# A transformer stack in split fp32: one weight tile of each stage multiplies old residual and new part apart, while the norm is made

## The chip, the cores and the metric

One core of a Trainium2 chip runs the whole network in one launch. TensorE (PE in the rows) multiplies, VectorE (DVE) and ScalarE (ACT) do the elementwise work, GpSimd (POOL) a few small steps, SyncE (SP) issues the loads of weights. The metric is the device time of one launch in microseconds, the median of several runs.

## What is computed

A batch of one, 256 tokens and 16 meta tokens (272 columns), a model width of 1024, depth 2. Layer 0: half-step SwiGLU, neighbourhood attention, half-step SwiGLU. Layer 1: the same with differential attention. Then a hybrid mixer (attention and an mLSTM side by side) and a squared-ReLU mlp. Every sublayer has a norm ahead and a norm behind:

```
def rmsnorm(x, g):
    xf = x.astype(jnp.float32)
    y = xf * lax.rsqrt(jnp.mean(xf * xf, axis=-1, keepdims=True) + RMS_EPS)
    return (y * g.astype(jnp.float32)).astype(x.dtype)

def swiglu(x, w_gate, w_up, w_down):
    return (jax.nn.silu(x @ w_gate) * (x @ w_up)) @ w_down

...
        f1 = swiglu(rmsnorm(h, g[0]), ffn_w_gate[i, 0], ffn_w_up[i, 0], ffn_w_down[i, 0])
        h = h + FFN_RES * rmsnorm(f1, g[1])
        j = i // N_MIXERS
        hn = rmsnorm(h, g[2])
```

The last lines tell the pattern: the residual h gets the sublayer's output, normed by its own mean square, and the next sublayer takes h, normed again.

## The kernel before, in words

The residual lies transposed, as `h[128, 8, 272]`: eight blocks of 128 features on the partitions, tokens on the columns (272 in the first four stages told of below, `ALL`; 256 behind them, `GRID`, where the meta tokens are no longer needed). Weights come as tiles of 128x1024 (one output block, eight input blocks) into `wr`. ACT rounds a tile to a high part `wh` (L156), DVE makes the remainder `wl` (L168). Inputs are split in the same way into `xh` and `xl`. A full product of an input block with a weight tile is three matmuls: wh·xh, wh·xl, wl·xh (L393 to L395); 24 for a tile. `W` is the ring of weight tiles: `W.next` takes one, `W.done` frees it, `W.pump`, `W.high` and `W.low_if` issue the loads and splits of coming ones at places in the program that are written by hand. The order on every engine is the order in which the code records the operations.

The norm ahead of a sublayer is not applied to its input. `xh` and `xl` hold g·h, the product is made with that, and the scale 1/rms, `rb`, is multiplied in when the product is taken out of PSUM. `rb` is needed only there, so its row sums (`Norm.head`) and transposes (`Norm.tail`) are put inside the next two gemms, behind a block that `first` and `second` name. The norm behind a sublayer is `Post`: `evac(ps, j)` takes the output of block j into `f` (times its gain) and adds its squares to a sum; `finish` makes the scale `bc` from it, by a ones-matmul over the partitions (L344), a mean (L356), a power on POOL (L349) and a transpose back (L368 to L373); then h += f·bc for each block (`addend` L617, `block` L623).

Between the last matmul of a sublayer and the first of the next stands this chain. `start_phase` is the piece of code for it, and it is called seven times: at about 214 us (neighbourhood mixer), 358 (ffn), 563 (ffn), 769 (differential mixer), 907 (ffn), 1099 (hybrid mixer) and 1236 us (mlp). While the chain runs, PE does idle matmuls on weights (`turn_over`, L476), nine between the row sums and the transposes, nine behind these. Then DVE forms block after block of h, ACT rounds it to `xh` (L436), DVE the low parts `xl` (L453), and PE multiplies four weight tiles block by block: for each block the high products of four tiles (L502, L503), at the end all low ones (L506): 4 x 24 = 96 matmuls. Behind them stand the sums of squares for `rb`.

The stages at 214, 563, 769 and 1099 follow `down`, the last gemms of an ffn: eight output blocks in pairs, each of three weight tiles. Those at 358, 907 and 1236 follow `proj_out`, which has one tile for each block, four blocks begun together as the attention's heads come out, and then the other four one by one. Attention's last steps stand in the code behind the start of `proj_out`, as it waits for its heads one by one.

Of the kernel before, what the change touches and what calls it, by code (L numbers as in the profile page):

```python
# [10 lines left out]
F32 = mybir.dt.float32  # L11
FR = mybir.dt.float32r
I32 = mybir.dt.int32
AF = mybir.ActivationFunctionType
# [7 lines left out]
T = S + NM  # L22
# [11 lines left out]
NK = NM + 4 * KC  # L34
HK = NK // 2
R_BUFS = 3


def constants():
# [170 lines left out]
def block_kernel(ctx: ExitStack, tc: tile.TileContext, a, out):  # L210
# [13 lines left out]
    def nm(s):  # L224
        uid[0] += 1
        return f"{s}_{uid[0]}"
# [149 lines left out]
    def square_into(acc, src, j, cols, bias=0.0, engine=dve):  # L376

        if j == 0:
            act.activation(acc[:, cols], src, AF.Square, bias=bias)
            return None  # L380
        q = tmp("sq")
        if j == NB - 1:
            x = cols.start
            for a, b in ((x, x + 128), (x + 128, T)):
                act.activation(q[:, a:b], src[:, a - x:b - x], AF.Square, bias=bias)
            return q
        act.activation(q[:, cols], src, AF.Square, bias=bias)  # L387
        engine.tensor_tensor(acc[:, cols], acc[:, cols], q[:, cols], op=OP.add)  # L388
# [34 lines left out]
    class Norm:  # L423


        def __init__(self, g, cols):
            self.g, self.cols = g, cols
            self.xh = bp.tile([128, 8, T], FR, name=nm("xh"), tag="xh", bufs=1)
            self.xl = bp.tile([128, 8, T], FR, name=nm("xl"), tag="xl", bufs=1)
            self.x = (self.xh, self.xl)  # L430
            self.acc = tp.tile([128, T], F32, name=nm("accp"), tag="acc", bufs=1)
# [6 lines left out]
        def square(self, j):  # L438
            c = self.cols
            q = square_into(self.acc, h[:, j, c], j, c, engine=pool)  # L440
            if q is not None:
                pool.tensor_tensor(self.acc[:, c], self.acc[:, c], q[:, c], op=OP.add)

        def sum(self, sq):

            c = self.cols
            dve.tensor_tensor(sq[:, 0:4, c], sq[:, 0:4, c], sq[:, 4:8, c], op=OP.add)
            dve.tensor_tensor(sq[:, 0:2, c], sq[:, 0:2, c], sq[:, 2:4, c], op=OP.add)
            dve.tensor_tensor(self.acc[:, c], sq[:, 0, c], sq[:, 1, c], op=OP.add)

        def low(self, j):
            c = self.cols
# [9 lines left out]
            act.activation(self.rb[:, self.cols], p[:, self.cols], AF.Copy)  # L462
            return self.rb

    def start_phase(norm, post, n=4):

        c = norm.cols
        w = [W.next() for _ in range(n)]  # L470
        ps = [ps_mm() for _ in range(n)]

        def turn_over(m):
            x = w[0][0].rearrange("p a b -> p (a b)")[:, 0:256]
            for _ in range(m):
# [3 lines left out]
        for k in range(2):  # L479
            act.activation(old[k][:, c], h[:, k, c], AF.Copy, scale=norm.g[:, k:k + 1])  # L480
        post.finish(turn_over)
        turn_over(9)
        t = []
        for k in range(2):
            t.append(post.addend(k))
            dve.scalar_tensor_tensor(norm.xh[:, k, c], t[k][:, c], norm.g[:, k:k + 1], old[k][:, c],
                                     op0=OP.mult, op1=OP.add)
        for k in range(2, 8):
            post.block(k)
            norm.block(k)  # L490
        for k in range(2):
            dve.tensor_tensor(h[:, k, c], h[:, k, c], t[k][:, c], op=OP.add)
        squares = post.f
        for x, y in ((2, 6), (6, 8), (0, 2)):
            act.activation(squares[:, x:y, c], h[:, x:y, c], AF.Square)
            if x:
                W.high()
        for k in range(8):
            norm.low(k)
        for k in range(8):  # L500
            for q in range(n):
                pe.matmul(ps[q][:, c], w[q][0][:, k, :], norm.xh[:, k, c], start=k == 0, stop=False)  # L502
                pe.matmul(ps[q][:, c], w[q][1][:, k, :], norm.xh[:, k, c], start=False, stop=False)  # L503
        for k in range(8):
            for q in range(n):
                pe.matmul(ps[q][:, c], w[q][0][:, k, :], norm.xl[:, k, c], start=False, stop=k == 7)  # L506
        W.low_if()
        norm.sum(squares)
        W.done(n)
        return ps  # L510

# [77 lines left out]
    class Post:  # L589


        def __init__(self, g, cols, bias=None, gbias=None):
            self.g, self.cols, self.bias, self.gbias = g, cols, bias, gbias
# [15 lines left out]
        def finish(self, between=lambda n: None):  # L609
            r = rstd_head(self.m, self.cols, self.sq)  # L610
            between(9)
            self.bc = rstd_tail(r, self.cols)

        def addend(self, j):
# [10 lines left out]
    def down(post, x_of, kbs):  # L625
        c = post.cols
        W.flush()
        for m2 in range(4):
            ps = [ps_mm(), ps_mm()]
            for n, kb in enumerate(kbs):  # L630
                last = n == len(kbs) - 1
                for q in range(2):
                    gemm(ps[q], x_of(n), c, kb, n == 0, last)
                    if last:
                        post.evac(ps[q], 2 * m2 + q)
                    if not (last and m2 == 3):
                        W.pump()
# [50 lines left out]
    def proj_out(post, x, order=range(8)):  # L688

        c = post.cols  # L690
        w = [W.next() for _ in range(4)]
        ps = [ps_mm() for _ in range(4)]
        for n, k in enumerate(order):
            while k not in ready:
                assert bg_list
                bg()
            W.flush()
            for q in range(4):
                mm3(ps[q][:, c], w[q], k, x, k, c, n == 0, n == 7)
# [189 lines left out]
        mask_bias(1)  # L889
        yield  # L890

    post = Post(half_gains(0, 1), ALL)
    bg_list.append(prepare())
    ffn(n0, post, (meta0, turn0, high0, keep0, gains_in, post.f), first_phase)

# [36 lines left out]
    QT = [slice(NM, NM + 128), slice(NM + 128, T)]  # L932


    norm = Norm(gains(0, 2), ALL)
    kq = slot(5, F32, "kq")
    Oh, Ol = slot(0, FR, "Oh"), slot(1, FR, "Ol")
    e_slot = slot(4, F32, "keep").rearrange("p a b -> p (a b)")
# [212 lines left out]
            mask_bias(2 + n // 8)  # L1151

    mixer(norm, post, na_evac, na_attention, ALL, na_before)
    post = Post(gains(0, 3), ALL, vgain("b_o"), gbo)
    proj_out(post, (Oh, Ol))


    norm = Norm(gains(0, 4), ALL)
    post2 = Post(half_gains(0, 5), ALL)
    t5b = []  # L1160

    def load_t5():
# [8 lines left out]

    bg_list.append(load_t5())
    ffn(norm, post2, post)
    norm = Norm(gains(1, 0), ALL)
    post = Post(half_gains(1, 1), ALL)
    ffn(norm, post, post2)


    norm = Norm(gains(1, 2), ALL)
    kq = slot(5, F32, "kq")  # L1180
    Oh, Ol = slot(0, FR, "Oh"), slot(1, FR, "Ol")
    keep_in(slot(3, F32, "keep"), slot(4, F32, "keep"))
# [109 lines left out]
                yield  # L1292

    mixer(norm, post, da_evac, da_attention, GRID, lambda n: None)
    post = Post(gains(1, 3), GRID)
    proj_out(post, (Oh, Ol))

    norm = Norm(gains(1, 4), GRID)
    post2 = Post(half_gains(1, 5), GRID)
    ffn(norm, post2, post)  # L1300


    norm = Norm(vgain("mix_pre"), GRID)
    Oh, Ol = slot(0, FR, "Oh"), slot(1, FR, "Ol")
    qk = slot(2, F32, "qk")
    vt = slot(3, F32, "vt")
# [11 lines left out]
    c = GRID  # L1318

    act.preload_act_table_set("natural_log_exp_and_others")  # L1320
    pg, *ps4 = start_phase(norm, post2)
# [244 lines left out]
    for n, (kind, i) in enumerate(plan):  # L1566
# [27 lines left out]
            bg_list.append(mlstm())  # L1594
            bg_list.append(causal_attention())
        bg()
    post = Post(vgain("mix_post"), GRID)
    proj_out(post, (Oh, Ol), [4, 5, 6, 7, 0, 1, 2, 3])


    norm = Norm(vgain("mlp_pre"), GRID)
    before = post
    uh = [slot(i, FR, "uh") for i in range(4)]
    ul = [slot(4 + i, FR, "ul") for i in range(4)]
# [117 lines left out]
```

## Time and profile before

| | |
|---|---|
| median of three runs | 1431.84 us (1429.91 to 1431.91) |
| the profiled run | 1431.22 us |
| its span, first to last instruction | 1429.4 us |
| PE busy | 1408.2 us, 99% |
| DVE busy | 893.7 us, 63% |
| ACT busy | 750.2 us, 52% |
| POOL busy | 168.1 us, 12% |
| mean granted TensorE clock | 0.998 |

Busy shares are means over the span. At the places that matter here PE's row of 99% holds the idle matmuls of the seven stages too, which are busy and do nothing. A time of one instruction is read with care where a row has several: they overlap, and the busy time over the count is the step from one to the next.

### The profile page before, as it was taken

How to read it: one execution, taken by the hardware profiler on the slowest of the kernel's cores; microseconds unless marked ns; L12 is line 12 of the kernel's file. 1: busy time of each engine (PE TensorE's matmuls, PEld its weight loads, DVE VectorE, ACT ScalarE, POOL GpSimd, SP SyncE). 2: the span in 40 equal slices, each digit the busy share in tenths (PEclk: the TensorE clock that was granted, in tenths of full speed). 3: DMA queues.
4: the chain of work that ended last, by engine and by line, in shares of the span. 5: the costliest groups of instructions: out<-in, count | busy, mean ns of one | idle time of the engine just before them, and what ended most of it. 6: DMA issues, size and time to landing. Idle time of an engine off the chain costs nothing.

```text
span 1429.4 us, 26895 instructions
## 1 busy us (share of the span) xinstructions
PE 1408.2 (99%) x11068; PEld 1357.6 (95%) x11068; DVE 893.7 (63%) x1668; ACT 750.2 (52%) x1333; POOL 168.1 (12%) x185
## 2 busy tenths in 40 slices
PE   9999999999999999999999999999999999999997
PEld 9999999899999999999999888999999888899886
DVE  6776447664865544955546785776555877686542
ACT  5554346666554444644445564664444565676441
POOL 1325001010221200212100001031100000000000
PEclk9999999999999999999999999999999999999999
DMA  7875552352575554555553352375554543275650
GB/s 250 271 251 172 179 185 66 124 167 90 167 229 172 168 180 148 175 180 177 163 182 99 119 177 89 112 244 184 188 178 131 177 129 108 89 234 179 221 177 30
DMA packets 219528, 234.41 MB, mean 164 GB/s; under 512 B 5313, under 2 KB 209894, under 8 KB 219214
## 3 DMA queue, kind: packets, MB, share of 16 engines
q1 hardware_dynamic: 218206, 227.38, 49.2%
q0 software_dynamic: 656, 4.94, 1.1%
q8 instruction: 87, 1.43, 0.4%
q10 hardware_dynamic: 544, 0.38, 0.1%
q14 instruction: 35, 0.29, 0.1%
HBM read 231.62 MB, written 5.13 MB: 166 GB/s over the span
## 4 chain that ended last, share of the span: by engine, by line
PE 91%; DVE 6%; ACT 2%; DMA 1%; issue 1%; POOL 0%; DVEq 0%; POOLq 0%; ACTq 0%; SPq 0%
PE pm L393 24%; PE pm L395 24%; PE pm L394 23%; PE ps L1645 2%; PE ps L1644 2%; PE ps L1646 2%; PE pm L506 2%; DVE wl L168 2%; PE pm L502 2%; PE pm L503 1%; DMA wr<-in_da_w_qkv_dram 1%; PE pt L344 1%; PE pt L1013 1%; PE pm L540 1%; PE ps L1022 1%
## 5 line engine op out<-in xcount | busy, mean ns | idle before, releaser
L168 DVE TENSOR_TENSOR wl<-wr,wh 128x1024 fp32r<-128x1024 f32 (+1 forms) x430 | 514.3, 1204 | 122.9 <-ACT wh L156 122.2
L393 PE MATMUL pm<-xh,wh 128*128 128x272 f32 (+1 forms) x1992 | 581.4, 292 | 2.2 <-DVE Ol L421 2.2
L395 PE MATMUL pm<-xh,wl 128*128 128x272 f32 (+1 forms) x1992 | 570.4, 286 | 0.0
L394 PE MATMUL pm<-xl,wh 128*128 128x272 f32 (+1 forms) x1992 | 568.5, 285 | 0.0
L156 ACT ACTIVATE wh<-wr 128x1024 fp32r<-128x1024 f32 (+1 forms) x430 | 440.7, 1033 | 194.0 <-PE pm L394 112.9
L393 PEld LDWEIGHTS pm<-xh,wh 128*128 128x128 f32 x1992 | 376.0, 189 | 11.2 <-issue 9.4
L395 PEld LDWEIGHTS pm<-xh,wl 128*128 128x128 f32 x1992 | 375.9, 189 | 0.1
L394 PEld LDWEIGHTS pm<-xl,wh 128*128 128x128 f32 x1992 | 375.6, 189 | 0.1
L395 PE MATMUL pm<-mh,wl 128*128 128x272 f32 (+1 forms) x704 | 202.2, 287 | 0.0
L393 PE MATMUL pm<-mh,wh 128*128 128x272 f32 (+1 forms) x704 | 202.1, 287 | 0.0
L394 PE MATMUL pm<-ml,wh 128*128 128x272 f32 (+1 forms) x704 | 201.5, 286 | 0.0
L650 POOL TENSOR_TENSOR sr<-sl,rb 128x272 f32<-128x272 f32 (+1 forms) x88 | 104.5, 1192 | 320.1 <-ACT sl L648 320.1
L395 PEld LDWEIGHTS pm<-mh,wl 128*128 128x128 f32 x704 | 132.7, 188 | 0.0
L394 PEld LDWEIGHTS pm<-ml,wh 128*128 128x128 f32 x704 | 132.6, 188 | 0.0
L393 PEld LDWEIGHTS pm<-mh,wh 128*128 128x128 f32 x704 | 132.6, 188 | 0.0
L420 ACT ACTIVATE mh<-m 128x272 fp32r<-128x272 f32 (+1 forms) x88 | 37.7, 428 | 117.8 <-DVE m L655 117.6
L655 DVE TENSOR_TENSOR m<-pm,sr 128x272 f32<-128x272 f32 (+1 forms) x88 | 38.3, 435 | 80.5 <-PE pm L395 74.8
L648 ACT ACTIVATE sl<-gq 128x272 f32<-128x272 f32 (+1 forms) x88 | 36.9, 427 | 95.8 <-DVE gq L646 95.6
L349 POOL TENSOR_TENSOR s<-s,mhalf 128x3 f32<-128x3 f32 (+1 forms) x15 | 19.1, 1274 | 558.4 <-DVE s L362 336.1
L646 DVE TENSOR_TENSOR gq<-pm,rb 128x272 f32<-128x272 f32 (+1 forms) x88 | 37.6, 435 | 71.6 <-PE pm L395 69.0
L388 DVE TENSOR_TENSOR accf<-accf,sq 128x272 f32<-128x272 f32 (+1 forms) x42 | 18.3, 436 | 81.9 <-ACT sq L387 81.8
L502 PE MATMUL pm<-xh,wh 128*128 128x272 f32 (+1 forms) x224 | 56.7, 291 | 0.6
(337 smaller groups left out, 1728.6 us busy)
## 6 DMA issues: line engine op xcount, KB each, us to landing
wr<-in_ffn_w_gate_dram SPq DMA_DIRECT2D x43, 1024.0 KB
wr<-in_ffn_w_up_dram SPq DMA_DIRECT2D x43, 1024.0 KB
wr<-in_ffn_w_down_dram SPq DMA_DIRECT2D x32, 1024.0 KB
wr<-in_w_up_dram SPq DMA_DIRECT2D x16, 1024.0 KB
wr<-in_w_down_dram SPq DMA_DIRECT2D x16, 1024.0 KB
wr<-in_ffn_w_down_dram SPq DMA_DIRECT2D x16, 768.0 KB
wr<-in_na_w_qkv_dram SPq DMA_DIRECT2D x12, 1024.0 KB
wr<-in_da_w_qkv_dram SPq DMA_DIRECT2D x12, 1024.0 KB
```

The costliest lines, as they stand in the source:

```text
L156: self.nc.scalar.activation(hi, w, AF.Copy)
L168: engine.tensor_tensor(lo, w, hi.bitcast(F32), op=OP.subtract)
L393: pe.matmul(ps, wh[:, k, :], xh[:, j, cols], start=start, stop=False)
L394: pe.matmul(ps, wh[:, k, :], xl[:, j, cols], start=False, stop=False)
L395: pe.matmul(ps, wl[:, k, :], xh[:, j, cols], start=False, stop=stop)
L420: act.activation(hi, src, AF.Copy)
L502: pe.matmul(ps[q][:, c], w[q][0][:, k, :], norm.xh[:, k, c], start=k == 0, stop=False)
L506: pe.matmul(ps[q][:, c], w[q][0][:, k, :], norm.xl[:, k, c], start=False, stop=k == 7)
L646: dve.tensor_tensor(t[:, c], ps[:, c], norm.rb[:, c], op=OP.mult)
L648: act.activation(s[:, c], t[:, c], AF.Silu)
L650: pool.tensor_tensor(s2[:, c], s[:, c], norm.rb[:, c], op=OP.mult)
L655: dve.tensor_tensor(t[:, c], ps[:, c], gated.pop(f)[:, c], op=OP.mult)
```

## The change

One of the four tiles of a stage, the `early` one (the first; in the hybrid mixer the second), takes its input blocks 0 to 3 in two terms. g·h_new is g·h_old + bc·(g·f), so W·(g·h_new) is W·(g·h_old) + bc·W·(g·f). Both products can be made before `bc` is known. `Norm.ahead` rounds and splits g·h_old of blocks 0 to 3 and g·f of blocks 0 to 3 into the columns of `xh` and `xl` that the stage fills later (blocks 0 to 3 and 4 to 7). PE makes 12 matmuls of the new part into a bank `term` and 12 of the old into the tile's own bank, in place of the 18 idle ones: 11 (256 columns: 10) between the row sums and the transposes, 10 behind these, the rest behind the first block. `term` is copied out by ACT, multiplied by `bc` and added at the end of the stage on DVE (`scaled`, `fb`). The early tile then needs only its blocks 4 to 7. So that these come first, the order of the blocks is 4, 5, 6, 7, 0, 1, 2, 3.

The copies and subtractions of h are recorded by `Post.next_norm`: in `down` at its second pair of blocks, in `proj_out` at its start. Those of f are recorded in `evac` behind blocks 4 and 5, two blocks each. A weight split (`W.low_if`) is recorded behind block 6. `head` moves from behind block 3 to behind block 6 of the first gemm after the stage, `tail` from block 1 to block 5 of the second. The new norm's sums of squares stand ahead of the stage's last weight split.

```
+ORDER = (4, 5, 6, 7, 0, 1, 2, 3)
+LOWS = (6, 7, 4, 5, 0, 1, 2, 3)
...
-            self.first, self.second = {3: self.head}, {1: self.tail}
+            self.first, self.second = {6: self.head}, {5: self.tail}
...
+        def ahead(self, j, src, x):
+            c = self.cols
+            act.activation(self.xh[:, x + j, c], src[:, j, c], AF.Copy, scale=self.g[:, j:j + 1])
+            dve.scalar_tensor_tensor(self.xl[:, x + j, c], src[:, j, c], self.g[:, j:j + 1],
+                                     self.xh[:, x + j, c].bitcast(F32), op0=OP.mult, op1=OP.subtract)
...
-    def start_phase(norm, post, n=4):
+    def start_phase(norm, post, n=4, early=0):
...
-        def turn_over(m):
-            x = w[0][0].rearrange("p a b -> p (a b)")[:, 0:256]
+        term = ps_mm()
+        def products():
+            for x, into in ((4, term), (0, ps[early])):
+                for k in range(4):
+                    for i, (part, v) in enumerate(((0, norm.xh), (1, norm.xh), (0, norm.xl))):
+                        pe.matmul(into[:, c], w[early][part][:, k, :], v[:, x + k, c],
+                                  start=k == 0 and i == 0, stop=x == 4 and k == 3 and i == 2)
+                        yield
...
-                pe.matmul(ps[0][:, 0:256], x[:, 0:128], x, start=True, stop=True)
...
-        post.finish(turn_over)
-        turn_over(9)
+        post.finish(lambda: some(11 if c is ALL else 10))
+        some(10)
+        scaled = tp.tile([128, T], F32, name=nm("fs"), tag="fs", bufs=1)
+        act.activation(scaled[:, c], term[:, c], AF.Copy)
...
+        def tiles(k):
+            return [q for q in range(n) if k > 3 or q != early]
...
+        high(ORDER[0])
+        some(24)
+        for k in ORDER[2:]:
             post.block(k)
             norm.block(k)
...
+        dve.tensor_tensor(scaled[:, c], scaled[:, c], post.bc[:, c], op=OP.mult)
...
+        for k in ORDER[1:]:
+            high(k)
...
+        norm.sum(squares)
         W.low_if()
-        norm.sum(squares)
+        x = tmp("fb")
+        dve.tensor_tensor(x[:, c], scaled[:, c], ps[early][:, c], op=OP.add)
+        ps[early] = x
...
+            if j in (4, 5):
+                for k in range(2):
+                    self.norm.ahead(2 * (j - 4) + k, self.f, 4)
+            if j == 6:
+                W.low_if()
+        def next_norm(self):
+            self.norm = Norm(self.gain, self.cols)
+            for j in range(4):
+                self.norm.ahead(j, h, 0)
...
+            if m2 == 1:
+                post.next_norm()
...
         ps = [ps_mm() for _ in range(4)]
+        post.next_norm()
```

On DVE, at the end of neighbourhood attention (330 us), the order before was this; `lg` and `s` are the masked logits and their maxima, `ps` the bank that PE filled, `Ol` the low part of a finished head.

```order
L421 TENSOR_TENSOR Ol_2578<-ps_4024,Oh_2577 128x256
L923 ISA lg_4141,s_4142<-ps_4134,bt_2770 128x176
L923 ISA s_4142 128x1
L923 ISA lg_4145,s_4146<-ps_4135,bt_2770 128x176
L923 ISA s_4146 128x1
```

and is now, the lines moved by the added code:

```order
L423 TENSOR_TENSOR Ol_2594<-ps_4040,Oh_2593 128x256
L451 SCALAR_TENSOR_TENSOR xl_4145<-h,G,xh_4144 128x272 x4
L968 ISA lg_4167,s_4168<-ps_4160,bt_2789 128x176
L968 ISA s_4168 128x1
L968 ISA lg_4171,s_4172<-ps_4161,bt_2789 128x176
L968 ISA s_4172 128x1
```

Four subtractions on h stand ahead of the last step of attention. On DVE at the end of the `proj_out` behind it (351 to 359 us) stood sums of squares (`accf`), weight splits (`wl`) and the mean of the row sums (`s`):

```order
L388 TENSOR_TENSOR accf_4123<-accf_4123,sq_4354 128x272
L168 TENSOR_TENSOR wl_4324<-wr_3953,wh_4323 128x1024
L168 TENSOR_TENSOR wl_4327<-wr_3953,wh_4326 128x1024
L388 TENSOR_TENSOR accf_4123<-accf_4123,sq_4393 128x272
L168 TENSOR_TENSOR wl_4360<-wr_4110,wh_4359 128x1024
L168 TENSOR_TENSOR wl_4366<-wr_4110,wh_4365 128x1024
L388 TENSOR_TENSOR accf_4123<-accf_4123,sq_4429 128x272
L356 TENSOR_SCALAR s_4459<-pt_4458 128x3
```

and now

```order
L390 TENSOR_TENSOR accf_4139<-accf_4139,sq_4380 128x272
L451 SCALAR_TENSOR_TENSOR xl_4145<-f_4138,G,xh_4144 128x272 x2
L170 TENSOR_TENSOR wl_4350<-wr_3969,wh_4349 128x1024
L170 TENSOR_TENSOR wl_4353<-wr_3969,wh_4352 128x1024
L390 TENSOR_TENSOR accf_4139<-accf_4139,sq_4423 128x272
L451 SCALAR_TENSOR_TENSOR xl_4145<-f_4138,G,xh_4144 128x272 x2
L170 TENSOR_TENSOR wl_4390<-wr_4126,wh_4389 128x1024
L170 TENSOR_TENSOR wl_4396<-wr_4126,wh_4395 128x1024
L390 TENSOR_TENSOR accf_4139<-accf_4139,sq_4463 128x272
L170 TENSOR_TENSOR wl_4433<-wr_4347,wh_4432 128x1024
L358 TENSOR_SCALAR s_4494<-pt_4493 128x3
```

Two pairs of subtractions on f stand between the sums, and one more weight split between the last sum and the mean.

## Rows read from the trace of the kernel before

**Rows 1.** The page's part 4: the chain of waits by engine, shares of the span.

```profile
PE 91%; DVE 6%; ACT 2%; DMA 1%; issue 1%; POOL 0%; DVEq 0%; POOLq 0%; ACTq 0%; SPq 0%
```

**Rows 2.** Groups by line and shape: count, busy us, mean ns, idle us before.

```profile
L476 PE MATMUL pm<-wh 128*128 128x256 f32 x126 | 18.4, 291 | 0.0
L453 DVE SCALAR_TENSOR_TENSOR xl<-h,G,xh 128x272 fp32r<-128x272 f32 x40 | 17.0, 496 | 0.0
L436 ACT ACTIVATE xh<-h,G 128x272 fp32r<-128x272 f32 x24 | 12.6, 524 | 22.7 <-DVE h L623 22.7
```

**Rows 3.** Timeline, stage at 563: start, length, operation, [idle before, releaser].

```profile
564.16 0.16 DVE L356 TENSOR_SCALAR s<-pt 128x3 f32<-128x3 f32 x1 [1.95 <-PE pt L344]
564.65 1.31 PE L476 MATMUL pm<-wh 128*128 128x256 f32 x9
...
567.67 0.39 PE L502 MATMUL pm<-xh,wh 128*128 128x272 f32 x1
...
576.12 4.15 PE L506 MATMUL pm<-xl,wh 128*128 128x272 f32 x32
...
580.11 0.29 PE L393 MATMUL pm<-xh,wh 128*128 128x272 f32 x1
```

**Rows 4.** Timeline, the last attention step before the `proj_out` of 344.

```profile
329.53 0.33 DVE L923 CUSTOM_DVE_ANT_0 lg<-ps,bt 128x176 f32<-128x176 f32 x1
...
330.00 0.57 ACT L1014 ACTIVATE ring<-pt 88x512 f32<-88x512 f32 x1
...
331.08 0.66 PE L1022 MATMUL ps<-ring,bt 88*64 88x128 f32 x8
```

**Rows 5.** Timeline, the end of that `proj_out` and the norm chain behind.

```profile
354.27 0.44 DVE L388 TENSOR_TENSOR accf<-accf,sq 128x272 f32<-128x272 f32 x1
...
354.63 2.36 DVE L168 TENSOR_TENSOR wl<-wr,wh 128x1024 fp32r<-128x1024 f32 x2
...
357.03 0.44 DVE L388 TENSOR_TENSOR accf<-accf,sq 128x272 f32<-128x272 f32 x1
...
357.79 0.72 PE L344 MATMUL pt<-ones,accf 128*128 128x1 f32 x6
...
358.55 0.16 DVE L356 TENSOR_SCALAR s<-pt 128x3 f32<-128x3 f32 x1 [1.08 <-PE pt L344]
...
360.55 0.32 PE L368 MATMUL pt<-ident,s 128*128 128x128 f32 x1
```

**Rows 6.** Timeline, the same two places ahead of the stage at 907.

```profile
878.86 0.44 DVE L923 CUSTOM_DVE_ANT_0 lg<-ps,t 128x272 f32<-128x272 f32 x1
...
880.16 0.83 PE L1240 MATMUL ps<-vs,ring 128*128 128x128 f32 x6
...
905.81 0.43 DVE L388 TENSOR_TENSOR accf<-accf,sq 128x256 f32<-128x256 f32 x1 [0.28 <-ACT sq L387]
...
906.65 0.50 PE L344 MATMUL pt<-ones,accf 128*128 128x1 f32 x4
```

**Rows 7.** Timeline, the same two places ahead of the stage at 1236.

```profile
1204.76 0.74 PE L1506 MATMUL ps<-qk 64*128 64x128 f32 x4
...
1235.73 0.54 PE L344 MATMUL pt<-ones,accf 128*128 128x1 f32 x4
```

**Rows 8.** Timeline, behind the stages at 214 and 1099.

```profile
235.80 0.40 ACT L462 ACTIVATE rb<-pt 128x272 f32<-128x272 f32 x1 [4.11 <-PE pt L370]
...
239.28 0.54 PE L988 MATMUL ps<-kq 64*128 64x160 f32 x4
...
1118.62 0.39 ACT L462 ACTIVATE rb<-pt 128x256 f32<-128x256 f32 x1 [2.50 <-PE pt L373]
```

**Rows 9.** PE's longest wait; windows: length, busy time (count) by engine, clock, DMA.

```profile
270.64 0.36 PE L393 MATMUL pm<-xh,wh 128*128 128x272 f32 x1 [2.19 <-DVE Ol L421]
...
272.00:275.00 3.00, 3.00 (x16) 2.92 (x14) 0.72 (x4) 0.90 (x3) 0.00 (x0) 0.50 0.69 233
...
1126.10:1127.60 1.50, 0.28 (x3) 0.08 (x2) 1.44 (x3) 0.00 (x0) 0.00 (x0) 1.00 1.00 313
```

More of the change, by code (lines that the diff above doesn't have):

```diff
@@ L436, in block @@
             act.activation(self.xh[:, j, c], h[:, j, c], AF.Copy, scale=self.g[:, j:j + 1])
[L438 to L442, printed above, removed]
         def sum(self, sq):
             c = self.cols
+            self.acc = tp.tile([128, T], F32, name=nm("accp"), tag="acc", bufs=1)
             dve.tensor_tensor(sq[:, 0:4, c], sq[:, 0:4, c], sq[:, 4:8, c], op=OP.add)
@@ L475, in turn_over, with some @@
+        todo = products()
+        def some(m):
             for _ in range(m):
-                pe.matmul(ps[0][:, 0:256], x[:, 0:128], x, start=True, stop=True)
+                next(todo, None)
         old = [tmp("go") for _ in range(2)]
-        for k in range(2):
-            act.activation(old[k][:, c], h[:, k, c], AF.Copy, scale=norm.g[:, k:k + 1])
-        post.finish(turn_over)
-        turn_over(9)
+        for i, k in enumerate(ORDER[:2]):
+            act.activation(old[i][:, c], h[:, k, c], AF.Copy, scale=norm.g[:, k:k + 1])
@@ L487, in start_phase, with high @@
                                      op0=OP.mult, op1=OP.add)
-        for k in range(2, 8):
+        def tiles(k):
+            return [q for q in range(n) if k > 3 or q != early]
+        def high(k):
+            for q in tiles(k):
+                pe.matmul(ps[q][:, c], w[q][0][:, k, :], norm.xh[:, k, c], start=k == 4 and q != early, stop=False)
+                pe.matmul(ps[q][:, c], w[q][1][:, k, :], norm.xh[:, k, c], start=False, stop=False)
+        high(ORDER[0])
+        some(24)
+        for k in ORDER[2:]:
@@ L489, in start_phase @@
             post.block(k)
             norm.block(k)
-        for k in range(2):
-            dve.tensor_tensor(h[:, k, c], h[:, k, c], t[k][:, c], op=OP.add)
         squares = post.f
-        for x, y in ((2, 6), (6, 8), (0, 2)):
+        for i, k in enumerate(LOWS):
+            if i == 2:
+                for x in range(2):
+                    dve.tensor_tensor(h[:, ORDER[x], c], h[:, ORDER[x], c], t[x][:, c], op=OP.add)
+            norm.low(k)
+        dve.tensor_tensor(scaled[:, c], scaled[:, c], post.bc[:, c], op=OP.mult)
@@ L495, in start_phase @@
+        for x, y in ((0, 4), (6, 8), (4, 6)):
             act.activation(squares[:, x:y, c], h[:, x:y, c], AF.Square)
-            if x:
+            if x != 4:
                 W.high()
[L498 to L503, printed above, removed]
@@ L504, in start_phase @@
-        for k in range(8):
-            for q in range(n):
-                pe.matmul(ps[q][:, c], w[q][0][:, k, :], norm.xl[:, k, c], start=False, stop=k == 7)
+        for k in ORDER[1:]:
+            high(k)
+        for k in LOWS:
+            for q in tiles(k):
+                pe.matmul(ps[q][:, c], w[q][0][:, k, :], norm.xl[:, k, c], start=False,
+                          stop=k == (5 if q == early else 3))
+        norm.sum(squares)
         W.low_if()
-        norm.sum(squares)
+        x = tmp("fb")
@@ L932, in block_kernel @@
     QT = [slice(NM, NM + 128), slice(NM + 128, T)]
-    norm = Norm(gains(0, 2), ALL)
+    norm = post.norm
     kq = slot(5, F32, "kq")
@@ L1153, in block_kernel @@
     mixer(norm, post, na_evac, na_attention, ALL, na_before)
[L1154 removed]
+    post = Post(gains(0, 3), ALL, gains(0, 4), vgain("b_o"), gbo)
     proj_out(post, (Oh, Ol))
[L1158 to L1159 removed]
+    norm = post.norm
+    post2 = Post(half_gains(0, 5), ALL, gains(1, 0))
     t5b = []
@@ L1173, in block_kernel @@
     ffn(norm, post2, post)
-    norm = Norm(gains(1, 0), ALL)
-    post = Post(half_gains(1, 1), ALL)
+    norm = post2.norm
+    post = Post(half_gains(1, 1), ALL, gains(1, 2))
     ffn(norm, post, post2)
-    norm = Norm(gains(1, 2), ALL)
+    norm = post.norm
     kq = slot(5, F32, "kq")
@@ L1320, in block_kernel @@
     act.preload_act_table_set("natural_log_exp_and_others")
-    pg, *ps4 = start_phase(norm, post2)
+    pg, *ps4 = start_phase(norm, post2, early=1)
     gi = cp.tile([128, 2, 36], F32, name="gi")
```

27 lines of the change are left out of this document (13 added, 14 removed).

## Prediction

> **What bounds the kernel now.** I read the page first: the chain of waits is TensorE (PE) for 91% of the span [rows 1], so a change pays only where it shortens PE's own stream or one of the few waits in it. Then I looked for what the removed matmuls occupy: the by-line view gives 126 idle matmuls, 18.4 us busy [rows 2]. They fill the time in which the norm of a stage's input is made, seven times, two groups of nine. That time is not PE's: in the stage at 563 us the first group starts at 564.65 and the first useful product only at 567.67 [rows 3], though two groups of 1.31 are 2.6; what sets it is the norm chain and not the filler. So the filler costs nothing; what can be won is useful work put in its place. Last I read the seven stages one after another, and before each the end of the stage ahead, since VectorE (DVE) and ScalarE (ACT) get new work there.
>
> I name the stages by their time: 214 (neighbourhood mixer), 358 and 563 (ffn), 769 (differential mixer), 907 (ffn), 1099 (hybrid mixer), 1236 (mlp). 358, 907 and 1236 follow a `proj_out`, which follows attention; the other four follow a `down`.
>
> **What it removes from PE.** The low products of 563 give the step: 32 in 580.11 - 576.12 = 3.99 us, 0.1247 us each [rows 3]. Before, the first useful product to the next gemm takes 580.11 - 567.67 = 12.44 us: 96 x 0.1247 = 11.97, and 0.47 of waits and pipeline. After, 24 products belong to the early tile, and it needs 12 matmuls fewer later; 21 of the 24 (20 where the stage has 256 columns) lie in the two gaps, 3 (4) behind the first block. Left is 96 - 12 + 3 = 87 (88) x 0.1247 = 10.85 us. The blocks' additions on DVE are then as early against PE as before, so I keep 0.1 us of wait of the 0.47. 12.44 - 10.95 is 1.5; the gaps hold 11 and 10 matmuls of 0.125 where nine of 0.13 stood (1.31 us a group, the last one's 0.28 among it), which I take as 0.05 later: **-1.45 us** for a clean stage, -1.57 at 358 and -1.43 in those with 256 columns by the same count.
>
> **What it adds.** Eight ACT copies and eight DVE subtractions a stage. One copy of this size is 0.52 us, one subtraction 0.50, but the subtractions run in rows of eight and overlap: 17.0 us busy for 40 of them, 0.425 each [rows 2]. For four copies in a row I take 0.42 too, by the same overlap, with 0.52 as the upper end. Four of each belong to h and need no result of the stage ahead, four to f as its blocks 0 to 3 are out. Where a `down` runs, long gemms of three weight tiles lie between two pairs of evacuations, and DVE stood idle for 1.95 us before the first step of the mean at 564.16 [rows 3]: this idle time hides them, and I cost them at nothing there (if it did not, four of 0.42 less the 1.95 would cost nothing either). At the end of a `proj_out` that cover is missing, and this is where the sum turns.
>
> *Attention's tail before `proj_out`.* The four on h are recorded at the start of `proj_out`, and DVE and ACT take them in that order, ahead of the last attention step. At 329.53 DVE starts the first mask-and-maximum (L923) of that step, and PE's product L1022 at 331.08 needs its bank free from these [rows 4]. After, ACT's four copies start behind the ring copy of 330.00, 0.57 long with some 0.1 of it overlapped [rows 4], at 330.5, and the last subtraction ends near 330.5 + 4 x 0.42 + 0.5 = 332.7. L923 comes behind it, and PE goes on at 333.1: **+2.0 us**. The same at 907: the second L923, 878.86, ends at 879.3, so four subtractions of 0.41 push it to some 880.75, and PE's L1240 from 880.16 [rows 6] to 880.76: **+0.6**. At 1236 it is ACT: four copies stand ahead of the copy that PE's L1506 at 1204.76 [rows 7] waits for: **+1.5**. The bounds are 0 (the four find a hole) and 2.2 (all four pairs one after the other).
>
> *The end of `proj_out`.* DVE's splits and sums stand there without a hole between them: a sum at 354.27, two splits from 354.63, the last sum of squares at 357.03, 0.44 long, and PE's row sums of it at 357.79 [rows 5]. PE's wait is 0.3 us from being real. Four subtractions there, and their wait for ACT's copies, put the sum at 359.05 and the row sums at 359.5. Then a weight split that used to stand behind the stage stands ahead of the mean (L356), as the order shows: 359.5 + 1.15 = 360.6 for a step that was at 358.55 [rows 5]. The chain behind it overlaps a little, so that the transposes of 360.55 come at 361.85: **+1.3**. At 907 the sum of 905.81 had 0.28 us of idle time ahead, PE's row sums follow at 906.65 [rows 6]: four subtractions of 0.41 less that hole, ACT's copies ahead of the first, and the split give **+1.15**. At 1236 the row sums of 1235.73 [rows 7] are moved in the same way: **+1.25**. Bounds: 0 and 1.9 (four subtractions plus the part of the split that shows).
>
> *The mixers.* A stage that ends earlier helps only if what follows is PE's. In the mixers, it is rb, the scale of the new norm, which DVE and ACT make and every evacuation needs: ready at 235.80 (214), 1118.62 (1099) [rows 8]. The sums of squares now come later against PE, since the order has fewer matmuls beside the same eight subtractions, and head and tail of the norm are moved by three and four blocks of the next gemm. By the order and the durations rb comes at 235.75 instead of 235.80, and at 1119.0 instead of 1118.6. At 214 PE's first score product stands at 239.28, and what it waits for descends from rb: I take **-1.0** of the 1.45. At 769 the same chain with less room: **-0.7**. At 1099 everything after rb is DVE's: **+0.2** (bounds for each: -1.45 and +0.4).
>
> *At no cost:* the squares on GpSimd that go were called nowhere; the sums of `term` and the early tile (three operations, each about as long as the sum of 0.44 in rows 5) fall in the last 5 us of the stage, where PE has its low products; a sixth buffer of products for `term` is free there because the attention's are out.
>
> **The sum.** 214: -1.0; 358: 2.0 + 1.3 - 1.57 = +1.7; 563: -1.45; 769: -0.7; 907: 0.6 + 1.15 - 1.43 = +0.3; 1099: +0.2; 1236: 1.5 + 1.25 - 1.43 = +1.3. Together +0.35 us on a profiled run of 1431.22 us (span 1429.4). The median of three runs is 1431.84; I set the sum on that: **1432.2 us**, no change that can be measured (0.2%, 2.9 us, is what can be told).
>
> **The rivals.**
> *The clock falls (slower).* PE's longest wait before is the one that ends at 270.64 after 2.19 us, and from 272 to 275 the granted clock is 0.50, that is 1.2 GHz: 3 us at half speed, 1.5 lost. In the 1.5 us of 1126.1 to 1127.6, in which PE was busy for 0.28, it stayed at 1.00 [rows 9]. The Trainium skill puts it as a rule ("TensorE: Matmul & The Clock Gate", section "What's actually happening"): the throttled clock is the default state, and only activity of TensorE lifts it, so a gap is paid twice, in waiting and in slow matmuls behind it. By that rule the trace agrees: 0.50 behind the wait of 2.19 us. The change opens new waits of 2.0 and 1.7 us at 358 and 1.1 to 1.5 at 907 and 1236; the first is close to the one that fell. Two falls are 3.0 us on top: 1435.2; three 1436.7. It decides from waits of about 2 us on: below that it is nothing.
>
> *The covers hold (faster).* ACT's and DVE's new work finds holes at the ends of `proj_out` too, and rb is no bound: 4 x 1.45 + 1.57 + 2 x 1.43 = 10.2 less: 1421.6. Against it stands the row of sums without a hole [rows 5]. If only the mixers gain in full and the three `proj_out` ends break even: 4 x 1.45 = 5.8 less, 1426.
>
> *It does not do what it says:* the early products' own inputs, the low parts of f's blocks 2 and 3, come after the last gemm, and the gap's matmuls wait for them instead of hiding. Then the stage gives nothing: 7 stages without gain and with the tails, 3.3 + 1.75 + 2.75 = 7.8 more, 1439.6. At a `down` this needs a subtraction to be two gemms late; I give it little.
>
> **How the numbers follow.** Forecast (gains at four stages and losses at three nearly cancel, 1429 to 1434.7): 0.46. The covers hold in part or full: 0.28. The clock or the waits make it dearer: 0.23; it doesn't do what it says: 0.03. So faster 0.28, same 0.46, slower 0.26. For 8 in 10 I go down to 1425.5, near the middle case of the covers, and up to 1437, with three falls, which also covers losses at their upper bounds (3 x 0.4 more at the mixers, 2.0 at the tails). The forecast's own range is 1429 to 1434.7.
>
> **What would show it.** In the trace of the changed kernel: 563 with 87 products in about 10.95 us from the first block's product to the next gemm (if 12, the blocks come late); PE waiting for DVE before the last attention step of 358 (2.0 us) and before the row sums at all three `proj_out` ends (1.1 to 1.7 us); rb at 214 and 1099 at the same time against the end of the stage ahead. I am wrong on the faster side if PE does not wait at those, on the slower if the granted clock is 0.50 in more than one stretch.

## The result and the profile after

The changed kernel takes 1439.05 us (1436.93 to 1440.07) against 1431.88 us: 1.0052 of the time before, 95% interval 1.0034 to 1.0069. It is slower by 7.2 us, outside the range of the forecast (1429 to 1434.7) and above the 1437 that the forecast gave as its wider upper end. The profiled run took 1438.45 us, its span is 1436.7 us.

The page of the changed kernel, part 1 (busy time and share by engine) and part 4 (the chain of waits), against [rows 1]:

```profile
PE 1405.2 (98%) x11026; PEld 1356.0 (94%) x11026; DVE 920.2 (64%) x1738; ACT 773.9 (54%) x1396; POOL 170.2 (12%) x185
...
PE 88%; DVE 7%; ACT 4%; issue 1%; POOL 0%; POOLq 0%; DVEq 0%; ACTq 0%
```

PE has 3.0 us less to do than before (1408.2) and the span is 7.3 us longer. PE's share of the chain fell from 91% to 88%, and DVE and ACT have the difference. So PE waits more. What it waits for stands in the view of the waits (engine, line and what was waited for: us in total, times, longest us), which has four new entries among its six largest:

```profile
PE pt L346 <- DVE accf L390: 3.9, 3, 1.6
PE ps L1067 <- DVE s L968: 2.0, 1, 2.0
...
PE ps L1551 <- ACT ring L1577: 1.5, 1, 1.5
...
PE pm L395 <- DVE s L968: 1.4, 1, 1.4
```

The first are the row sums at the end of the three `proj_out`s, the others the last steps of the three attentions: 8.8 us at places where PE did not wait before.

The second new thing is the granted clock. Windows of the changed kernel (window: length, busy PE (count), granted clock, DMA share, GB/s):

```profile
361.00:364.00 3.00, 3.00 (x16) 0.50 0.85 294
...
1211.00:1214.00 3.00, 3.00 (x15) 0.50 0.00 0
...
1245.00:1248.00 3.00, 3.00 (x16) 0.50 0.78 269
```

Three stretches at 1.2 GHz, each some 2 us behind the end of a new wait (those of 359.35, 1208.47 and 1242.8). The stretch of the kernel before, 272 to 275 [rows 9], is at full clock now.

Both programs issue the same 8664 matmuls of the ordinary gemms in the same order, so each can be paired with its own, and the difference of their starts be read at any place. What is added to it (us) in each stretch, here for the kernels of the experiments as well:

```
before, us    place                     forecast  after   e1     e2     e4     e9
   0-  31     load, first stage             -     +0.5   -0.9   +0.6   +0.4   +0.6
 207- 267     stage 214, mixer behind     -1.0    -0.1   -0.2   +0.1   -0.3   -0.1
 267- 290     attention, the wait of 268    -     -2.7   -2.8   -1.6   -2.7   -2.7
 290- 356     its tail                    +2.0    +2.1    0.0   +2.1   +2.1    0.0
 356- 563     proj_out's end, stage 358   -0.3    +1.9   +0.1   +3.4   +0.4   +0.4
 563- 760     stage 563                   -1.45   -1.0   -1.3    0.0   -1.0   -1.0
 760- 873     stage 769, mixer behind     -0.7    -0.2   -0.5   -0.3   -0.1   -0.1
 873- 905     attention's tail            +0.6    +1.4    0.0   +1.4   +1.4    0.0
 905-1098     proj_out's end, stage 907   -0.3    +0.2    0.0   +1.4   +0.2   +0.2
1098-1199     stage 1099, mixer behind    +0.2    +0.1   +0.2    0.0   +0.2   +0.1
1199-1235     mixer's tail                +1.5    +3.6    0.0   +3.5   +5.0   +0.1
1235-1331     proj_out's end, stage 1236  -0.2    +1.4    0.0   +1.3   +0.1   +0.6
sum                                       +0.35   +7.2   -5.5  +12.0   +5.7   -2.1
```

The first line differs from run to run by about 1 us either way with the first loads, and is no effect of an edit. Each column is one profiled run. A time of one trace is set beside a time of another only after the lines above it are taken off: at 329 us, for instance, the changed kernel runs 2.3 us ahead of the one before.

### The profile page after: what moved, and what is told of

Read it like the earlier page. It is cut to its first block, busy times and chain, and to the rows that moved or that the text cites. A ratio compares the mean times of both kernels' runs of the same rounds, so it can differ in the third digit from the quotient of the medians.

```text
span 1436.7 us, 27037 instructions
## 1 busy us (share of the span) xinstructions
PE 1405.2 (98%) x11026; PEld 1356.0 (94%) x11026; DVE 920.2 (64%) x1738; ACT 773.9 (54%) x1396; POOL 170.2 (12%) x185
## 4 chain that ended last, share of the span: by engine, by line
PE 88%; DVE 7%; ACT 4%; issue 1%; POOL 0%; POOLq 0%; DVEq 0%; ACTq 0%
PE pm L395 23%; PE pm L397 22%; PE pm L396 22%; DVE wl L170 3%; PE ps L1690 2%; PE ps L1689 2%; PE ps L1691 2%; PE pm L510 2%; PE pm L534 2%; PE pm L511 2%; PE pm L482 1%; ACT wh L158 1%; PE pt L346 1%; PE ps L1285 1%; ACT keep L971 1%
## 5 line engine op out<-in xcount | busy, mean ns | idle before, releaser
L395 PE MATMUL pm<-xh,wh 128*128 128x272 f32 (+1 forms) x1992 | 581.1, 292 | 1.3 <-DVE Ol L423 1.1
L395 PE MATMUL pm<-Oh,wh 128*128 128x256 f32 (+1 forms) x192 | 56.9, 296 | 1.8 <-DVE s L968 1.4
```

Of the source, the lines that this page charges most:

```text
L395: pe.matmul(ps, wh[:, k, :], xh[:, j, cols], start=start, stop=False)
```

## The experiments

The theory after the result: the loss is made at the ends of attention and of `proj_out`, where DVE and ACT take the new work ahead of steps that PE waits for, and by the clock, which falls behind such waits. The rival: it is spread over all seven stages, by the moved row sums, the later scale `rb` and the extra work.

**Half of the change.** In `e1_down_only` the stages behind a `proj_out` are as before, in `e2_proj_only` the ones behind a `down`:

```
     def start_phase(norm, post, n=4, early=0):
+        if not post.parts:
+            return old_phase(norm, post, n)
...
-        post.next_norm()
+        post.next_norm(False)      # e1: in proj_out; e2: in down
```

> The change undone at the three stages behind a proj_out (358, 907, 1236 are as before, with their idle matmuls); kept at the four behind a down. Theory: the loss is made at the ends of attention and proj_out and by the clock that falls behind those waits. Then the three low stretches of the granted clock at 361, 1211 and 1245 are gone and the waits of PE for accf, for the maxima and for the ring copy with them; left are the shifts that the two traces show at the other stages: +0.4 at the start, 0.0 at 214, -1.0 at 563, -0.1 at 769, +0.3 at 1099, and -2.6 at 268 if the clock stays up there: 1429 us (1428 to 1432). Rival: the loss comes from the moved row sums and the late scale at all stages, or from the extra work as such; then it stays above 1434.

> The other half: the change undone at the four stages behind a down, kept at the three behind a proj_out. Theory: it holds nearly the whole loss: shifts of +2.0 and +1.8 at 330 and 358, +1.4 and +0.1 at 880 and 907, +3.5 and +1.4 at 1205 and 1236, together 10.2: 1442 us, or 1439 to 1440 if the clock falls once less. Rival (loss spread over all stages): near 1435.

Measured: e1 1426.83 us, 0.997 of before (0.9958 to 0.9983), faster; e2 1441.4 us, 1.0072 (1.0057 to 1.0087). The halves lie 14.6 us apart, and the whole loss is in e2. In e1 the four new waits are gone and the granted clock is 1.00 until past 1410 us. The rival falls. But e1's 5.5 us are not all the edit's purpose: 2.8 of them are the wait at 268, of which more below, and 0.9 the first loads; the stages themselves give 1.9.

**The attention tails.** `e3_late_h` records h's four copies and subtractions behind attention's last step:

```
         ps = [ps_mm() for _ in range(4)]
-        post.next_norm()
...
         ready.clear()
+        post.next_norm()
         W.done(4)
```

> The change with the four copies and subtractions of h recorded behind attention's last step in proj_out, ahead of its evacuations, where DVE and ACT idled for 7 us before. Theory: the three waits in attention's tail go (2.0 + 1.4 + 1.9 us) and with the third the clock's fall behind it (1.6): 1432 us; the waits before the row sums and their clock falls stay. Rival: DVE and ACT are the bound for the added work wherever it stands, so it comes back at the evacuations: 1437 or more.

Measured: 1432.63 us, 1.0009 (0.9999 to 1.002). The three tails added 2.1, 1.4 and 3.6 us; here each adds nothing (0.0 in the trace). The mechanism can be read in the trace of the changed kernel (timeline: start, length, operation, [idle before, releaser]):

```profile
328.19 1.75 ACT L450 ACTIVATE xh<-h,G 128x272 fp32r<-128x272 f32 x4
...
328.74 1.74 DVE L451 SCALAR_TENSOR_TENSOR xl<-h,G,xh 128x272 fp32r<-128x272 f32 x4 [1.40 <-ACT xh L450]
330.39 0.33 DVE L968 CUSTOM_DVE_ANT_0 lg<-ps,bt 128x176 f32<-128x176 f32 x1
...
330.88 1.09 PE L1067 MATMUL ps<-ring,bt 88*64 88x128 f32 x16 [2.02 <-DVE s L968]
```

DVE sat idle for 1.40 us, because the first subtraction waits for ACT's first copy and nothing behind it in DVE's queue may pass; then the four take 1.65 us; then comes L968, which PE is waiting for (in [rows 4] it had started at 329.53, which is 327.2 here, with PE going on at 331.08, here 328.8). What e3 does not repair is the clock: all three ends of `proj_out` have a low stretch in its trace, at 358, 912 and 1242, where the changed kernel had two. And a fall can last longer than those three: at 358 both of these windows of e3 are at half clock,

```profile
358.00:361.00 3.00, 3.00 (x15) 0.50 0.97 290
361.00:364.00 3.00, 3.00 (x16) 0.50 0.18 59
```

and the stage adds 3.4 us, as it does in e2. In the change the fall at this place is half as long, and the stage adds 1.9.

**The clock.** `e4_fill` shortens no wait. It puts 12 idle matmuls (9 in the stages of 256 columns) between the last gemm of a `proj_out` and the row sums:

```
             gemm(p, x, c)
+            if j == 7:
+                scrap = ps_mm()
+                for _ in range(12 if c is ALL else 9):
+                    pe.matmul(scrap[:, 0:256], post.norm.xh[:, 0, 16:144], post.norm.xh[:, 0, 16:272], start=True, stop=True)
             post.evac(p, j)
```

> The change with idle matmuls (12, in stages of 256 columns 9) recorded on PE between the last gemm of a proj_out and the row sums, in the time that PE waits there for the sum of squares. They shorten no wait. Theory: the clock falls at 361 and 1245 because of that wait, so with PE busy the granted clock stays at 1.00 there and about 1.6 us come back for each: 1436 us. Rival: the loss is the wait itself, and the low clock costs nothing beside it: 1439.

Measured: 1436.45 us, 1.0036 (1.0019 to 1.0052), as the theory said. Its six single times lie between 1432.5 and 1441.2, so that the median alone would not settle it; the traces do. The timeline of e4 at the end of the first `proj_out`, and the same windows as above:

```profile
357.31 1.60 PE L762 MATMUL pm<-xh 128*128 128x256 f32 x12
359.08 0.83 PE L346 MATMUL pt<-ones,accf 128*128 128x1 f32 x6 [0.17 <-DVE accf L390]
...
360.09 0.15 DVE L358 TENSOR_SCALAR s<-pt 128x3 f32<-128x3 f32 x1
...
361.92 0.27 PE L370 MATMUL pt<-ident,s 128*128 128x128 f32 x1
```

```profile
361.00:364.00 3.00, 3.00 (x26) 1.00 0.84 295
...
1211.00:1214.00 3.00, 3.00 (x16) 0.50 0.00 0
...
1245.00:1248.00 3.00, 3.00 (x25) 1.00 0.67 236
```

The row sums start at 359.08 (359.35 in the changed kernel), so the wait for the sum of squares is as long as it was. But PE is busy in it, the clock stays at 1.00 at both places, and 26 matmuls run in the 3 us in which 16 ran. The stages at 358 and 1236 add 0.4 and 0.1 us where they added 1.9 and 1.4: **1.3 to 1.5 us for a fall**. At 1211, where nothing was filled, the clock is as low as before, and from an earlier time on (it is at 0.50 from 1208 too), so that this tail adds 5.0 where it added 3.6. In the Trainium skill ("TensorE: Matmul & The Clock Gate", section "What's actually happening") activity is what releases the throttle; e4 is that statement in one edit, since the activity here is work of no use.

**Both repairs.** `e9_late_fill` is e3 and e4 in one kernel.

> Both single repairs in one kernel: h's copies and subtractions behind attention's last step, and the idle matmuls ahead of the row sums. Theory: the loss is the tails (2.0 + 1.4 + 1.9 us) and the falls of the clock (about 1.5 us each, three), and nothing else of size; then 1439.05 - 5.3 - 4.5 = 1429.2, the granted clock stays at 1.00 at all three stages, and these stages end where those of the kernel before do. Rival: the two repairs overlap or something third is left: 1432 or more.

Measured: 1429.0 us (1427.3 to 1429.2), 0.9977 (0.9968 to 0.9986). The forecast sum, 1439.05 - 5.3 - 4.5 = 1429.2, is met within 0.2 us. In its trace the only stretch below full clock is at the very end, the waits for `accf`, the maxima and the ring are not among the ten largest, and the ten times lie within 2 us, where those of e3 spread over 5. So tails and falls account for the loss. What is left is not the gain that was sought: without the -2.7 of 268 and the +0.6 of the first loads, e9's column adds up to nothing.

**The moved row sums.** `e5_head_back` puts the row sums and transposes of the next norm back to where they were (`{3: self.head}, {1: self.tail}`).

> The change with the row sums and the transposes of the next norm back behind block 3 of the first gemm and block 1 of the second, as before. The sums of squares end 2.0 us after the stage's end now (1.0 before). Theory: then PE waits for the sums and for the power on GpSimd, some 0.5 and 1.1 us at each stage, and the mixers at 214, 769 and 1099 get their scale at most 0.6 us earlier: slower than the change, 1442 to 1447. Rival: the moved steps are themselves what ate the gain at 214, 769 and 1099 (0.9, 1.6 and 1.5 us by the shift between the traces) and at the start (0.4): 1435.

Measured: 1444.47 us, 1.0088 (1.0072 to 1.0105): slower by 5.4 than the change. Its view of the waits has a new line:

```profile
PE pt L346 <- DVE accp L445: 2.4, 5, 0.6
```

PE now waits five times for the sums, about 0.5 us each, as expected; the waits for the power, expected at 1.1 us a stage, are 0.7 us in two. The rest goes with further and longer falls of the clock (five low stretches before 1400 us, where the change has three). At 214 and 769 the rival is right in part: they are 0.4 and 0.5 us better than in the change. Moving them was right in the sum, but by how much? `e8_down_54` is e1 with `{5: self.head}, {4: self.tail}` for the stages behind a `down`.

> The change at the four stages behind a down alone (1426.8 us), with the row sums behind block 5 and the transposes behind block 4. Theory: as in the kernel above, 1 to 1.5 us less: 1425.5. Rival: the same or slower.

Measured: 1425.56 us, 0.9959 (0.9944 to 0.9974). That is 1.3 us under e1 by the medians; the traces show -0.5 against -0.2 at 214 and -0.9 against -0.5 at 769, and nothing at 1099, so 0.7 us of it has a place. It has the lowest median of the study, but its times (1424.8 to 1426.4) overlap those of e1 (1425.6 to 1427.4).

**The way that failed.** `e6_late_soon` was to make the ends of `proj_out` gain: h late, f's copies and subtractions behind the evacuations of blocks 1 and 3, and no weight split behind block 6.

```
-            if j in (4, 5):
+            if self.soon and j in (1, 3):
+                for k in (j - 1, j):
+                    self.norm.ahead(k, self.f, 4)
+            if not self.soon and j in (4, 5):
...
-            if j == 6:
+            if not self.soon and j == 6:
                 W.low_if()
```

> At the proj_outs, h's copies and subtractions stand behind attention's last step, f's right behind the evacuations of blocks 1 and 3 (where DVE idled for 1.2 us and more in the old trace), and the weight split ahead of the mean goes. Theory: then nothing queues ahead of the sums of squares, PE's waits before the row sums go and the clock stays up; each of the three stages gains about 1.4 us as those behind a down do at their own end: 1422 to 1424. Rival: DVE and ACT are full at the end of a proj_out whatever the order, so that the row sums still come a microsecond late: 1427 or more.

Measured: 1449.64 us, 1.0116 (1.0087 to 1.0145), against 1422 to 1424 expected. Two lines of its waits, and two rows of ACT and PE at the first `proj_out`:

```profile
PE pm L397 <- DVE wl L170: 11.0, 7, 2.9
PE pt L346 <- DVE accf L390: 7.6, 3, 3.4
```

```profile
357.19 1.06 ACT L158 ACTIVATE wh<-wr 128x1024 fp32r<-128x1024 f32 x1 [2.99 <-DMA wr<-in_ffn_w_gate_dram]
...
359.16 1.44 PE L346 MATMUL pt<-ones,accf 128*128 128x1 f32 x6 [3.36 <-DVE accf L390]
```

`e7_soon_54`, the same with the row sums at 5 and 4, fared alike.

> The last kernel, and the row sums behind block 5 and the transposes behind block 4 of their gemms (6 and 5 in the change). In the trace of the change PE reaches block 6 some 0.3 us after the sums are ready and block 5 of the second gemm 0.5 us after the power is. Theory: the scale comes 0.4 to 0.6 us earlier at 214, 769 and 1099, and nothing waits elsewhere: 1 to 1.5 us faster than without. Rival: DVE's order (a weight split ahead of the mean) sets the scale and PE waits at the earlier place: same or up to 1 us slower.

Measured: 1445.92 us, 1.0104 (1.0083 to 1.0124). `e10_soon_split` has the split of block 6 back.

> e6_late_soon (1449.6 us) with the weight split behind block 6 of a proj_out put back. There PE waited 11.0 us for weight splits and 7.6 for sums of squares. Theory: the missing split put every later split one place back, so that the first tiles of the next gemms came late: with it the 11 us go, and what stays is the later sums: 1434 to 1438. Rival: the early subtractions of f delay the release of the raw weights and so the loads, and that is the cost: 1445 or more.

Measured: 1437.33 us, 1.0038 (1.0024 to 1.0052). The 11.0 us of waits for weight splits are gone, the ones for `accf` are 7.1 us. So the missing split cost some 12 us; that every split behind it came one place later than the tile was wanted is the reading, and is not shown by itself. And the early subtractions do not help, for a reason that the row of ACT shows: at the end of `proj_out` the weights themselves are late. ACT waits 2.99 us for a load, and the squares of block 6 stand behind that in its queue. A load can only be issued when a split has freed the buffer, and subtractions ahead of the split delay it. The split and the load behind it, in e3 and then in e6 (the two run within 0.2 us of each other here):

```profile
346.87 1.22 DVE L170 TENSOR_TENSOR wl<-wr,wh 128x1024 fp32r<-128x1024 f32 x1
348.16 0.37 SPq L107 DMA_DIRECT2D wr<-in_ffn_w_gate_dram  x1
...
349.17 1.22 DVE L170 TENSOR_TENSOR wl<-wr,wh 128x1024 fp32r<-128x1024 f32 x1
350.46 0.37 SPq L107 DMA_DIRECT2D wr<-in_ffn_w_gate_dram  x1
```

The load is issued 0.07 us behind the end of the split in both, and 2.3 us later in e6. In these kernels DVE's order there is bound on both sides: behind the split the sum is late (e3), ahead of it the load (e6, e10).

## Why the prediction was wrong

The forecast was a sum of +0.35 us. By the table the profiled run has +7.2. Step by step:

*What held.* The places and the causes. PE waits before the last attention step of 358 for L923's results, 2.0 us forecast, 2.02 in the trace; it waits before the row sums of all three `proj_out`s, 1.1 to 1.7 us forecast, 1.6, 1.2 and 1.1 measured (3.9 in three). The stage behind a `down` is shorter, and 1099 gains nothing (+0.2 forecast, +0.1). The figure of the third rival, 1439.6, is near the time measured by accident: PE waits for none of the early products' inputs.

*The step that failed first: the clock was left out of the sum.* I made the sum at full clock and kept the falls as a rival with a chance of 0.23, though the sum itself opened six new waits of 0.6 to 2.0 us, and [rows 9] showed what one of 2.19 had done. Three of the six were followed by a fall, of 1.46 (358, against e4), 1.29 (1236, against e4) and some 1.6 us (behind 1205: 3.6 less the 2.0 by which PE is late ahead of the low stretch; filling that wait was not tried). That is 4.4 us; without it the time would lie just inside the range. The rival's condition failed with it: it was to decide from waits of about 2 us on and to be nothing below, and the three waits were of 1.6, 1.1 and 1.5 us, while the one of 2.0 had no fall. The rival gave 1436.7 for three; three came, and its sign (0.50 in more than one stretch), but at 1439.05, for the terms below. Which waits are followed by a fall is not a matter of length alone, and this stays open: the wait of 2.02 us at 329 and the one of 1.21 at 909 are followed by none in the changed kernel, but the same two waits have one in e5 (0.50 from 330.5 to 333.5) and in e2 and e3; and in e2 the wait of 268, 2.19 us as before, is followed by full clock:

```profile
271.34 0.36 PE L395 MATMUL pm<-xh,wh 128*128 128x272 f32 x1 [2.19 <-DVE Ol L423]
...
272.00:275.00 3.00, 3.00 (x27) 1.00 0.93 316
```

The spread of single times goes with the falls: 1430.1 to 1434.9 in e3, with them (mean granted clock 0.994 in the three longest runs, 0.996 in the five shortest), and 1427.3 to 1429.2 in e9, without.

*Terms that were mis-sized: the clean stage.* Forecast -1.45 at 563, measured -0.97. The rows that answer to [rows 3], in the trace of the changed kernel:

```profile
569.45 0.34 PE L510 MATMUL pm<-xh,wh 128*128 128x272 f32 x1
...
570.15 0.50 DVE L502 SCALAR_TENSOR_TENSOR xh<-hb,G,go 128x272 fp32r<-128x272 f32 x1 [0.46 <-DVE hb L659]
...
572.15 0.39 PE L510 MATMUL pm<-xh,wh 128*128 128x272 f32 x1
...
577.27 3.67 PE L534 MATMUL pm<-xl,wh 128*128 128x272 f32 x28
...
580.78 0.29 PE L395 MATMUL pm<-xh,wh 128*128 128x272 f32 x1
```

and the same places in e1, whose code for this stage is the same:

```profile
563.96 0.34 PE L512 MATMUL pm<-xh,wh 128*128 128x272 f32 x1
...
564.31 0.50 DVE L504 SCALAR_TENSOR_TENSOR xh<-hb,G,go 128x272 fp32r<-128x272 f32 x1
...
574.92 0.29 PE L395 MATMUL pm<-xh,wh 128*128 128x272 f32 x1
```

From the first useful product of a finished block to the next gemm it is 580.78 - 569.45 = 11.33 us in the changed kernel, and 574.92 - 563.96 = 10.96 in e1, where 10.95 were forecast. The count of 87 matmuls and the 0.1 us of wait were right; what the changed kernel has on top is a hole on DVE, 0.46 us ahead of its second block (none in e1), after which PE catches up with the blocks (the row of 572.15 begins 0.38 behind its predecessor, where the step is 0.125). The hole stands at 563 and at 769 in the change, e3, e4, e5, e9 and e10, and in neither place in e1, e6, e7 and e8, which have no weight split behind block 6 of `proj_out`; what DVE waits for there the trace does not say, since the step named had long ended. In both the change and e1 the useful work in the gaps makes the stage begin 0.14 later behind the row sums, not 0.05. Without the hole the stage gives -1.34 (563 in e1) and -1.36 (214 in the change).

*The mixers.* Forecast -1.0 and -0.7 at 214 and 769, measured -0.1 and -0.2. At 214 the stage itself ends 1.36 us earlier, and the gain goes behind it, in two steps. The scale stands at 236.41 where [rows 8] has 235.80; 0.47 of that is the first line of the table, so that it came 0.14 later and not, as I had worked out, 0.05 earlier. The chain to it in the changed kernel:

```profile
231.46 0.44 DVE L445 TENSOR_TENSOR accp<-f 128x272 f32<-128x272 f32 x1
...
232.56 0.72 PE L346 MATMUL pt<-ones,accp 128*128 128x1 f32 x6
...
233.32 0.16 DVE L358 TENSOR_SCALAR s<-pt 128x3 f32<-128x3 f32 x1
...
233.57 1.76 POOL L351 TENSOR_TENSOR s<-s,mhalf 128x3 f32<-128x3 f32 x1 [16.50 <-DVE s L358]
...
235.87 0.27 PE L370 MATMUL pt<-ident,s 128*128 128x128 f32 x1
...
236.41 0.40 ACT L465 ACTIVATE rb<-pt 128x272 f32<-128x272 f32 x1 [4.70 <-PE pt L372]
```

The sums are ready at 231.9, the row sums come 0.7 us later because PE is at block 6 only then, the mean waits for the addition `fb` in DVE's queue (no idle time ahead of it), and the power is done at 235.33 while PE is not at block 5 of its gemm until 235.87. I had the durations, but not these places. Behind the score products that need the scale, 0.57 us of the gain is left. e8 moves both one block forward and has 0.97 left there. The second step has no term in the sum. It is a wait of PE that was not there before, and it takes another 0.5:

```profile
260.71 0.64 PE L1058 MATMUL pt<-ident,keep 128*88 128x128 f32 x4 [0.36 <-ACT bt L1079]
```

At 769 it goes the same way: 1.0 won by the stage, 0.9 given back at the scores, 0.6 more at 806.35, where PE's wait for ACT's `vs` has grown from 0.31 to 0.90 us, and 0.7 won back behind that.

*The end of `proj_out`.* The row sums came where the forecast put them, and so did the mean: in e4, at full clock, 359.08 and 360.09, with this part of the launch 0.47 us ahead of the kernel before, which makes them 1.8 and 2.0 later than in [rows 5]. But the transposes (361.92) are then 1.84 later and not 1.3: the 0.7 us that I let the chain overlap are not there. The other two ends were not taken apart in this way.

*The tails.* Forecast 0.6 at 907, measured 1.4: PE's wait is not at L1240 but, earlier, at a product of `proj_out` (880.89, 1.36 us of wait, ended by the mask step L968); and my own terms, 879.3 and four of 0.41, put the end of the mask step at 880.9 and not 880.75. Forecast 1.5 at 1236, measured 2.0 before the clock.

*What was not in the sum at all.* -2.7 us at 268: the wait of 2.19 us became 1.1, since one weight split now stands ahead of the step that PE waits for, where two stood before. The splits in the kernel before and in the changed one, and in the changed one also the product of PE that waited:

```profile
268.05 2.35 DVE L168 TENSOR_TENSOR wl<-wr,wh 128x1024 fp32r<-128x1024 f32 x2
...
268.47 1.22 DVE L170 TENSOR_TENSOR wl<-wr,wh 128x1024 fp32r<-128x1024 f32 x1
...
269.93 0.36 PE L395 MATMUL pm<-xh,wh 128*128 128x272 f32 x1 [1.05 <-DVE Ol L423]
```

The fall behind it is gone too, 1.6 of the 2.7 by e2. The change moved the splits by one place, and here that was luck: without it the loss would have been 9.9 us. The sum of all: 0.35 forecast, + 4.4 (clock) + 1.9 (stages behind a `down`) + 1.4 (tails) + 1.4 (ends of `proj_out` at full clock, 0.4, 0.2 and 0.1 against -0.3, -0.3 and -0.2) - 2.7 (268) + 0.5 (first line of the table) = 7.25. It closes because each term is read from the table against the forecast; the experiments, not the closing, are what shows the causes of the first and the third.

## What to carry to other kernels

Work that is hoisted to be ready early is paid in the queues that it is hoisted into: an engine takes its operations in order, so ask of each recorded operation which result behind it TensorE is waiting for at that moment, and move it to where that engine idles. Where the same edit is made at several places, cost each on its own and keep those that pay: here the four behind a `down` alone (e8) are 0.4% faster than before. Of e8's 5.3 us, though, 2.7 are the luck of 268; of the stages, 563 gives 1.3, 769 0.9, 214 0.5 and 1099 nothing. And where a wait of TensorE of a microsecond or more is opened, put the price of a clock fall into the sum and not beside it.

## What the runs showed of the hardware that was not expected

A wait of TensorE of 1.1 us was followed by a granted clock of 0.50 (1242 in the changed kernel, and not in e4, where the wait was filled), and the same wait of 2.19 us is followed by a fall in one kernel and by none in another (268 in before and e2). A fall costs 1.3 to 1.6 us here, more where the low stretch is longer (3.4 us added by the stage at 358 in e2 and e3, 1.9 in the change, 0.4 with no fall in e4), and idle matmuls in the wait prevent it at no other cost: 12 of them, with the wait as long as it was, took 1.5 us off the stage at 358.
